# 160 instead of 128 tokens by gathered expert rows, the second expert product with its table rows stationary, and wide table tiles

## The chip, the cores and the metric

The kernel runs on one core of one Trainium2 chip. The metric is the device time of one execution in microseconds (us). Engines are named as in the profile: PE is TensorE, DVE VectorE, ACT ScalarE, POOL GpSimd, SP the queue of SyncE that issues the ordinary loads. GpSimd issues the gathers.

## What is computed

One layer of a decoder trunk on 512 tokens of 2048 features. A first part (norm, attention and linear attention heads, output projection) gives `x`. The second part is a mixture of 16384 experts of one neuron each, and a final norm:

```python
def peer_ffn(h, w_q, sub_keys, u_tab, v_tab):
    q = (h @ w_q).reshape(B, S, PEER_HEADS, 2, PEER_HALF)
    s = jnp.einsum('bshpd,hpkd->bshpk', q, sub_keys)
    top_s, top_i = lax.top_k(s, PEER_TOPK)
    ...
    expert = i1 * PEER_NKEYS + i2
    gate = jax.nn.softmax(best_s, axis=-1)
    ...
        u = jnp.take(u_tab, et, axis=0)
        act = jax.nn.gelu(jnp.einsum('td,ted->te', xt, u), approximate=False)
        return jnp.einsum('te,ted->td', gt * act, jnp.take(v_tab, et, axis=0))
```

Each token has 8 heads with 16 experts each, so 128 experts of the 16384. A row of `u_tab` and of `v_tab` is 2048 float32, 8 KB. The result is rmsnorm(x + g2 * peer_ffn(h)), with `g2` from the conditioning vector ("ada" sections below).

## The kernel before

**Two ways through the experts.** The first 128 tokens, one on each partition, go the gathered way. For each of their 128 expert slots GpSimd gathers 128 rows of `u_rows` (1 MB, one row for each token), VectorE multiplies them by the tokens' h and sums (`dot`), 16 slots at a time get gelu and gate (`weigh`), and then rows of `v_rows` are gathered, scaled and added up by VectorE (`add`). That makes 256 gathers, each followed by one VectorE instruction over 2048 columns. Three buffers `gat` go round. A gather is held back until ScalarE has cast a certain tile of `v_rows` (`pace[0]`).

The other 384 tokens go the dense way, through all 16384 experts, of which those that were not chosen have gate 0. The experts are taken in 128 groups of 128, a group being called j:

- `product1(j)` computes h times u for one j. Four table tiles of `u_t`, each 128x512 float32 (256 KB), are loaded by SP into `wraw` (six buffers). ScalarE casts each to its high part `whi`, VectorE subtracts to get the low part `wlo` (`split`; both have four buffers). TensorE then makes for each of 16 feature blocks three passes (high x high, high x low, low x high) with a 128x128 piece of the table stationary and the 384 tokens as moving columns: 48 passes of 384 columns. ScalarE's gelu puts the sum into `wt`.
- `gate(j)` multiplies `wt` by the dense gate matrix (`gtile`, read back from DRAM) on VectorE, casts the high part on ScalarE and subtracts the low part on VectorE.
- `product2(j, half)` multiplies these token weights by rows of the v table: the token weights are stationary (three blocks of 128 tokens) and 512 features move. For both halves of the features a j has 36 passes of 512 columns. Its v tiles are 128x512 too, loaded and split in the same way.

**The loop.** Chunks of `CH` = 4 j: for one half of the features, the four j are summed in six PSUM banks, then for the other half, and `evacuate` adds the six banks onto `xo` on VectorE; the half that ends a chunk stays in PSUM and begins the next chunk. Within every second step one more `product1` is made ahead (`next1`), and a step of the gathered way is taken (`sparse_some`). The engines' instruction streams are fixed when the program is built, by a scheduler that follows priorities and the buffers of the pools; on the chip every engine works through its own stream in order, and waits for semaphores.

**Around it.** Before the loop the top 16 of each head are found on VectorE, 14 first products are made ahead, and the dense gate matrix is generated in 12 blocks of 32 tokens: VectorE makes one-hot matrices, TensorE multiplies them, ScalarE copies them out (`stg`), and 2 MB of each block go to DRAM (`gd`). One section of the conditioning ("late ada", 64 tiles of 128x512 through `wraw`, summed by VectorE at L214) is worked off within the loop by `advance`. In the tail the last half is finished with v tiles split in advance (`stage`), GpSimd multiplies by `g2` and adds x (`onto_x1`, `other_half`), and the norm and the output follow token block by token block.

Of the kernel before, what the change touches and what calls it, by code (L numbers as in the profile page):

```python
# [21 lines left out]
P = 128  # L22
# [10 lines left out]
NDB = 3  # L33
NT = NDB * P
GT = 32
GJ = 4
CH = 4
NADA = 6
NWRAW = 6
# [3 lines left out]
RAW = 16  # L43
NPRE = 3
# [30 lines left out]
def hybrid_layer(ctx, tc, a, out):  # L75
# [49 lines left out]
    G1 = const.tile([P, KD], F32, name="G1")  # L125
    stat = const.tile([P, 5, 48], F32, name="stat")

    def rstd(dst, ss, n, width):
        v, y, z = stat[:, 1, :n], stat[:, 2, :n], stat[:, 3, :n]
# [25 lines left out]
    x1d = dram.tile([TB, P, D], F32, name="x1d")  # L155
# [496 lines left out]
    ws = pools.push("ws", LEFT, bufs=4)  # L652
# [20 lines left out]
    def first_heads(f):  # L673
        b = sums1[f] = bank(f"o{f // 2 % 2}")
        w = [load_w(ws, a["w_out"][f][:, k0:k0 + 4, :], [P, 4, P]) for k0 in (8, 12)]
        for ks, part, x in ((korder[:8], 0, mhi), (korder[:8], 1, mhi), (korder[:8], 0, mlo)):
            for k in ks:
                mm(b, w[k // 4 - 2][part][:, k % 4, :], x[k], start=x is mhi and part == 0 and k == 8, stop=False)

    for f in range(KD):  # L680
# [5 lines left out]
        for ik, k0 in enumerate((0, 4)):  # L686
            wh, wl = load_w(ws, a["w_out"][f][:, k0:k0 + 4, :], [P, 4, P])
            for j in range(4):
                mm3(b, wh[:, j, :], wl[:, j, :], mhi[k0 + j], mlo[k0 + j], False, k0 + j == 7)
            if f >= EWAIT:  # L690
                advance(2 + ik)
        x1f = x1T[:, f, :]
        nc.vector.scalar_tensor_tensor(out=x1f, in0=b, scalar=G1[:, f:f + 1], in1=x1f, op0=OP.mult, op1=OP.add)
        add_square(x1p, total, x1f, f == 0, nc.gpsimd if f < KD - 1 else nc.vector)
# [5 lines left out]
    h2 = [h2p.tile([P, TB, KD, P], F32R, name=n) for n in ("h2hi", "h2lo")]  # L700
# [4 lines left out]
    for k in range(KD):  # L705
# [3 lines left out]
        t4 = t.rearrange("p (a b) -> p a b", a=TB)  # L709
# [3 lines left out]
    for tb in range(TB):  # L713
        x1 = x1p.tile([P, D], F32, name="x1", tag="x1", bufs=2)
        for k4 in range(4):
            b = bank("tr")
            for j in range(4):
                nc.tensor.transpose(out=b[:, j * P:(j + 1) * P], in_=x1T[:, k4 * 4 + j, tb * P:(tb + 1) * P],
                                    identity=ident)
            nc.scalar.copy(out=x1[:, k4 * 512:(k4 + 1) * 512], in_=b)  # L720
        nc.sync.dma_start(out=x1d[tb], in_=x1)
# [6 lines left out]

    rp = pools.push("retr", RIGHT, bufs=2)
# [15 lines left out]
    for h in range(8):  # L745
        tv = rp.tile([P, 2, TB, 16], F32, name="tv", tag="tv")
        ti = rp.tile([P, 2, TB, 16], U32, name="ti", tag="ti")
        for p2 in range(2):
# [3 lines left out]
            b4 = b.rearrange("p (a b) -> p a b", a=TB)  # L752
            for k0 in range(0, KD, 4):
                wh, wl = load_w(ws, a["w_q"][f][:, k0:k0 + 4, :], [P, 4, P], "gpsimd")
                for j in range(4):
# [38 lines left out]
    def product1(j, lo_eng):  # L794
        b = bank("p1")
        b3 = b[:, :NT].rearrange("p (a b) -> p a b", a=NDB)
        wt = upl.tile([P, NT], F32, name="wt", tag="wt")
        for k0 in range(0, KD, 4):
# [9 lines left out]

    def next1(lo_eng="vector"):
        j = next(todo1, None)  # L810
# [15 lines left out]
    ef = slp.tile([P, P], F32, name="ef")  # L826
    flat = [[ids[:, tb, p2].rearrange("p h s -> p (h s)") for p2 in range(2)] for tb in range(TB)]
    nc.vector.scalar_tensor_tensor(out=ef, in0=flat[0][0], scalar=128.0, in1=flat[0][1], op0=OP.mult, op1=OP.add)
    nc.vector.tensor_copy(out=eidx, in_=ef)
    nc.vector.tensor_copy(out=gate0, in_=gates[:, 0].rearrange("p h s -> p (h s)"))  # L830
    slot = slp.tile([P, 4, NT], F16, name="slot")
    gres = slp.tile([P, NT], F32, name="gres")
    for tb in range(1, TB):
        for n, src in enumerate((flat[tb][0], flat[tb][1], gates[:, tb].rearrange("p h s -> p (h s)"))):
            b = bank("sk")
            nc.tensor.transpose(out=b[:, 0:P], in_=src, identity=ident)
            tsl = slice((tb - 1) * P, tb * P)
            if n == 2:
                nc.scalar.activation(gres[:, tsl], b[:, 0:P], AF.Copy, scale=GATE_UP)
            else:  # L840
                nc.scalar.copy(out=slot[:, n, tsl], in_=b[:, 0:P])
# [5 lines left out]
    for k4 in range(4):  # L847
        b = bank("pj")
        for j in range(4):
            k = k4 * 4 + j  # L850
            for n, src in enumerate(h2):
                mm(b[:, j * P:(j + 1) * P], src[:, 0, k, :], identr, start=(j == 0 and n == 0),
                   stop=(j == 3 and n == 1))
        nc.scalar.copy(out=h2s[:, k4 * 512:(k4 + 1) * 512], in_=b)
# [46 lines left out]
    act0 = sp.tile([P, P], F32, name="act0", bufs=1)  # L901
    wt0 = sp.tile([P, P], F32, name="wt0", bufs=1)
    nc.gpsimd.memset(acc0, 0.0)

# [298 lines left out]
```

## Time and profile before

| | |
|---|---|
| time, median of 3 runs (lowest to highest) | 3340.71 us (3340.18 to 3340.81) |
| profiled execution: its time, its span | 3344.42 us, 3342.7 us |
| busy in the span: PE, DVE, ACT, POOL | 95%, 75%, 37%, 27% |
| moved by DMA | 786.36 MB, 235 GB/s on average |
| granted TensorE clock, mean | 0.983 of full speed |

The span is what the profiler saw from the first instruction to the last. Busy times of TensorE overlap, since passes are pipelined: the distance between two starts is what a pass costs, not its duration. The other engines' instructions overlap slightly at their ends, too.

### The profile page before, as it was taken

To read this page: it belongs to the slowest core of one execution; us is meant where nothing else is said; L and a number is where in the kernel's file an instruction comes from. 1 tells how busy PE (TensorE), PEld (TensorE's weight loads), DVE (VectorE), ACT (ScalarE), POOL (GpSimd) and SP (SyncE) were. 2 spreads that over 40 slices of the span, in tenths; PEclk is the share of its full clock that TensorE was granted. 3 is DMA by queue.
4 is the path that set the end of the run, shared out by engine and by line. 5 is a ranking of instruction groups with operands and counts; after the bars stand their busy time and mean duration, and the time that the engine had idled before them with its cause. 6 is when DMAs were issued, how large, how long until landed. Compare 5 with 4: busy or idle time off the path is not lost. (4 is left out here: it accounts for less than half of the span.)

```text
span 3342.7 us, 46002 instructions
## 1 busy us (share of the span) xinstructions
PE 3173.7 (95%) x16009; PEld 2749.5 (82%) x16009; DVE 2523.7 (75%) x3989; ACT 1252.2 (37%) x2152; POOL 901.6 (27%) x630
## 2 busy tenths in 40 slices
PE   3999999999997889999999999999999999999997
PEld 2777786688786778988888888898888899999985
DVE  8988846674899885777777777777777777777777
ACT  3333354523422773333333333333333333333333
POOL 6554411111454462212211111112111111111123
PEclk9999999999998999999999999999999999999998
DMA  7876720184322468888888888888888888888864
GB/s 228 277 237 216 260 92 19 38 298 135 136 89 76 178 232 269 294 287 285 291 286 292 289 290 286 282 293 273 289 283 296 276 297 281 277 273 286 280 204 141
DMA packets 343817, 786.36 MB, mean 235 GB/s; under 512 B 33624, under 2 KB 108024, under 8 KB 307616
## 3 DMA queue, kind: packets, MB, share of 16 engines
q1 hardware_dynamic: 305600, 511.75, 47.3%
q0 software_dynamic: 37984, 271.68, 21.7%
q8 instruction: 125, 2.05, 0.2%
q14 instruction: 108, 0.88, 0.1%
HBM read 749.73 MB, written 33.56 MB: 234 GB/s over the span
## 5 line engine op out<-in xcount | busy, mean ns | idle before, releaser
L102 ACT CAST whi<-wraw 128x512 fp32r<-128x512 f32 (+1 forms) x779 | 477.2, 615 | 873.1 <-PE b_p L97 439.7
L97 PE MATMUL b_p<-h2hi,wlo 128*128 128x384 f32 x2048 | 695.0, 339 | 26.8 <-DVE wlo L103 19.7
L95 PE MATMUL b_p<-h2hi,whi 128*128 128x384 f32 x2048 | 692.6, 338 | 18.9 <-ACT whi L102 18.9
L96 PE MATMUL b_p<-h2lo,whi 128*128 128x384 f32 x2048 | 691.6, 338 | 0.0
L96 PE MATMUL b_p<-wlo,h2hi 128*128 128x512 f32 x1512 | 594.1, 393 | 10.7 <-DVE wlo L994 10.7
L97 PE MATMUL b_p<-whi,h2lo 128*128 128x512 f32 x1512 | 593.1, 392 | 0.0
L95 PE MATMUL b_p<-whi,h2hi 128*128 128x512 f32 x1512 | 589.5, 391 | 0.4 <-DVE xo L1022 0.2
L993 ACT CAST whi<-wraw 128x512 fp32r<-128x512 f32 x504 | 313.4, 623 | 684.8 <-PE b_p L96 537.1
L994 DVE TENSOR_TENSOR wlo<-wraw,whi 128x512 fp32r<-128x512 f32 x504 | 362.8, 725 | 273.4 <-ACT whi L993 271.5
L103 POOL TENSOR_TENSOR wlo<-wraw,whi 128x512 fp32r<-128x512 f32 (+1 forms) x259 | 410.8, 1595 | 416.7 <-ACT whi L102 385.8
L103 DVE TENSOR_TENSOR wlo<-wraw,whi 128x512 fp32r<-128x512 f32 x520 | 349.6, 689 | 124.9 <-ACT whi L102 124.5
L97 PEld LDWEIGHTS b_p<-h2hi,wlo 128*128 128x128 f32 x2048 | 386.8, 189 | 36.6 <-DVE wlo L103 27.4
L95 PEld LDWEIGHTS b_p<-h2hi,whi 128*128 128x128 f32 x2048 | 387.7, 189 | 24.2 <-ACT whi L102 19.2
L914 POOL DMA_INDIRECT gat<-in_u_rows,eidx x128 | 185.3, 1448 | 785.5 <-ACT whi L993 696.2
L96 PEld LDWEIGHTS b_p<-h2lo,whi 128*128 128x128 f32 x2048 | 387.2, 189 | 4.5
L914 POOL DMA_INDIRECT gat<-in_v_rows,eidx x128 | 161.9, 1265 | 802.5 <-ACT whi L993 688.5
L96 PEld LDWEIGHTS b_p<-wlo,h2hi 128*128 128x128 f32 x1512 | 285.2, 189 | 71.6 <-DVE wlo L994 14.5
L95 PEld LDWEIGHTS b_p<-whi,h2hi 128*128 128x128 f32 x1512 | 285.4, 189 | 61.6 <-issue 4.1
L97 PEld LDWEIGHTS b_p<-whi,h2lo 128*128 128x128 f32 x1512 | 285.4, 189 | 59.5
L214 DVE SCALAR_TENSOR_TENSOR acc<-adaw,cact,acc 128x512 f32<-128x512 f32 (+1 forms) x330 | 311.1, 965 | 22.4 <-DMA adaw<-in_ada_w 17.7
L928 DVE SCALAR_TENSOR_TENSOR acc<-gat,wt,acc 128x2048 f32<-128x2048 f32 x128 | 300.3, 2346 | 12.8 <-DMA gat<-in_v_rows,eidx 12.8
L920 DVE SCALAR_TENSOR_TENSOR gat<-gat,h2s 128x2048 f32<-128x2048 f32 x128 | 292.0, 2285 | 13.5 <-DMA gat<-in_u_rows,eidx 13.5
(359 smaller groups left out, 4185.2 us busy)
## 6 DMA issues: line engine op xcount, KB each, us to landing
wraw<-in_u_t SPq DMA_DIRECT2D x512, 256.0 KB, 4.2
wraw<-in_v_rows SPq DMA_DIRECT2D x512, 256.0 KB, 5.3
adaw<-in_ada_w SPq DMA_DIRECT2D x224, 256.0 KB, 4.3
adaw<-in_ada_w SPq DMA_DIRECT2D x128, 192.0 KB, 3.4
gd<-stg SPq DMA_DIRECT2D x12, 2048.0 KB, 7.3
gtile<-gd SPq DMA_DIRECT2D x32, 768.0 KB, 8.7
wraw<-in_w_out SPq DMA_DIRECT2D x64, 256.0 KB, 4.1
wraw<-in_w_q SPq DMA_DIRECT2D x64, 256.0 KB, 2.6
```

The lines of the kernel that those rows point to most:

```text
L95: mm(o, wh, xh, start=first, stop=False)
L96: mm(o, wh, xl, start=False, stop=False)
L97: mm(o, wl, xh, start=False, stop=last)
L102: nc.scalar.copy(out=hi, in_=src)
L103: (nc.vector if lo_eng == "vector" else nc.gpsimd).tensor_tensor(out=lo, in0=src, in1=hi, op=OP.subtract)
L214: nc.vector.scalar_tensor_tensor(out=acc, in0=w[:, j, :], scalar=cact[:, k:k + 1], in1=acc, op0=OP.mult, op1=OP.add)
L914: ins = nc.gpsimd.indirect_dma_start(out=g, out_offset=None, in_=a[table], in_offset=bass.IndirectOffsetOnAxis(ap=eidx[:, s:s + 1], axis=0))
L920: after(nc.vector.scalar_tensor_tensor(out=g, in0=g, scalar=1.0, in1=h2s, op0=OP.mult, op1=OP.mult, accum_out=act0[:, s:s + 1]), pace[1], ...
L928: after(nc.vector.scalar_tensor_tensor(out=acc0, in0=g, scalar=wt0[:, s:s + 1], in1=acc0, op0=OP.mult, op1=OP.add), pace[1], ORDER)
L993: pace[0] = nc.scalar.copy(out=vh, in_=vr).ins.name
L994: pace[1] = nc.vector.tensor_tensor(out=vl, in0=vr, in1=vh, op=OP.subtract).ins.name
```

## The change

- **Tokens.** 32 more tokens go the gathered way. Their slots are packed: 32 tokens on each quarter of the partitions, four of their 128 slots at once, so that they take 32 further slots of 128 rows (`eidxb`, `gateb`, `h2sb`, `accb`). That makes 160 slots and 320 gathers. The dense way has 352 tokens, in 11 groups of 32; h is stored in 16 groups of 32 tokens, so that the moving operand of `product1` is read in 11 runs of 32 columns, where it was read in 3 runs of 128.
- **Second product.** `product2(pair, g)` now holds 128x128 pieces of the v table stationary and moves the 352 token weights, as the first product does. The features are taken in four groups of 512 (`g`), each of four PSUM banks, and the result lies by features. A j has 48 passes of 352 columns here, and 96 in all.
- **Tiles.** All table tiles are 128x1024 (512 KB), of u, v (from a copy of the table in the order of its use, `v_t`), and of two projections ahead. `whi` and `wlo` have two buffers each, `wraw` three.
- **Loop.** Two chunks of four and twenty of six j; in each chunk four feature groups of two or three pairs, of which the first three are evacuated. 20 first products are made ahead of the loop.
- **Around it.** The gate matrix has 11 blocks. 16 copies on ScalarE put h of the gathered tokens in order. Only the 160 gathered tokens' x is transposed to rows. In the tail, x and `g2` are added on VectorE, blocks of the result are transposed back to rows, and the four copies of the 32 tokens are summed by a small matmul.

```diff
-NDB = 3
-NT = NDB * P
+NB = 32
+NA = P + NB
+NT = T - NA
+NQ = NT // GT
-CH = 4
+CHUNKS = (4, 4) + (6,) * 20
+NSLOT = 7
+NHOST = 8
+DG = 4
+PER1, PER2 = 1.42, 0.71
-NWRAW = 6
+NWRAW = 3
-RAW = 16
-NPRE = 3
+RAW = 12
+NPRE = 8
...
-    ws = pools.push("ws", LEFT, bufs=4)
+    ws = pools.push("ws", LEFT, bufs=2)
...
     def product1(j, lo_eng):
         b = bank("p1")
-        b3 = b[:, :NT].rearrange("p (a b) -> p a b", a=NDB)
-        wt = upl.tile([P, NT], F32, name="wt", tag="wt")
-        for k0 in range(0, KD, 4):
-            uh, ul = load_w(ws, a["u_t"][j][:, k0:k0 + 4, :], [P, 4, P], lo_eng)
-            for kk in range(4):
+        b3 = b[:, :NT].rearrange("p (a b) -> p a b", a=NQ)
+        wt = xo[:, j if j < DG else KD - NHOST + j, :] if j < NHOST else upl.tile([P, NT], F32, name="wt", tag="wt")
+        for k0 in range(0, KD, 8):
+            uh, ul = load_w(ws, a["u_t"][j][:, k0:k0 + 8, :], [P, 8, P], lo_eng)
+            for kk in range(8):
                 k = k0 + kk
-                mm3(b3, uh[:, kk, :], ul[:, kk, :], h2[0][:, 1:, k, :], h2[1][:, 1:, k, :], k == 0, k == KD - 1)
+                mm3(b3, uh[:, kk, :], ul[:, kk, :], h2[0][:, GA:, k, :], h2[1][:, GA:, k, :], k == 0, k == KD - 1)
...
-        for s0 in range(0, P, 16):
+        for s0 in list(range(P, NA, 16)) + list(range(0, P, 16)):
             for table, f in (("u_rows", dot), ("v_rows", add)):
...
+    def product2(pair, g, banks, first, last):
+        vr = ws.tile([P, 2, 512], F32, name="wraw", tag="wraw", bufs=NWRAW)
+        nc.sync.dma_start(out=vr, in_=a["v_t"][pair][g])
+        vh = ws.tile([P, 2, 512], F32R, name="whi", tag="whi")
+        vl = ws.tile([P, 2, 512], F32R, name="wlo", tag="wlo")
+        pace[0] = nc.scalar.copy(out=vh, in_=vr).ins.name
+        pace[1] = nc.vector.tensor_tensor(out=vl, in0=vr, in1=vh, op=OP.subtract).ins.name
+        for jj in range(2):
+            wh, wl = wpair[pair * 2 + jj]
+            for dc in range(DG):
+                dsl = slice(dc * P, (dc + 1) * P)
+                mm3(banks[dc][:, :NT], vh[:, jj, dsl], vl[:, jj, dsl], wh, wl, first and jj == 0, last and jj == 1)
+    def evacuate(g, banks):
+        for dc in range(DG):
+            o = xo[:, g * DG + dc, :]
...
+                nc.vector.tensor_tensor(out=o, in0=banks[dc][:, :NT], in1=o, op=OP.add)
...
+    for c, n in enumerate(CHUNKS):
+        order = range(DG) if c % 2 == 0 else range(DG - 1, -1, -1)
...
+        for p, g in enumerate(order):
...
+            for i in range(n // 2):
+                if step % 2 == 1:
+                    n1 = done1[0]
+                    next1()
+                    sparse_some(PER1 * (done1[0] - n1))
+                if c > 1 and step % 2 == 0:
+                    advance()
+                product2(j0 // 2 + i, g, banks, i == 0 and (p > 0 or c == 0), i == n // 2 - 1 and
+                         (p < DG - 1 or c == last_c))
+                if p == DG - 1 and c < last_c:
+                    gate(j0 + n + CHUNKS[c + 1] * (i + 1) // (n // 2) - gated[0])
+                sparse_some(PER2)
+                step += 1
...
+            elif p < DG - 1:
+                evacuate(g, banks)
```

Where instructions stand is shown at two places. The first is VectorE's stream in the loop, around an evacuation. Before, it reads so (`wlo` of L994 is a v tile's low part and of L103 a u tile's; L928 adds a gathered slot; L1022 evacuates a bank onto `xo`):

```order
L994 TENSOR_TENSOR wlo_22540<-wraw_22537,whi_22539 128x512
L928 SCALAR_TENSOR_TENSOR acc0_11141<-gat_22408,wt0_11143,acc0_11141 128x2048
L994 TENSOR_TENSOR wlo_22570<-wraw_22567,whi_22569 128x512
L994 TENSOR_TENSOR wlo_22585<-wraw_22582,whi_22584 128x512
L1022 TENSOR_TENSOR xo_11146<-b_p2_21956,xo_11146 128x512
L1022 TENSOR_TENSOR xo_11146<-b_p2_21957,xo_11146 128x512
L1022 TENSOR_TENSOR xo_11146<-b_p2_21958,xo_11146 128x512
L1022 TENSOR_TENSOR xo_11146<-b_p2_21959,xo_11146 128x512
L1022 TENSOR_TENSOR xo_11146<-b_p2_21960,xo_11146 128x512
L1022 TENSOR_TENSOR xo_11146<-b_p2_21961,xo_11146 128x512
L928 SCALAR_TENSOR_TENSOR acc0_11141<-gat_22441,wt0_11143,acc0_11141 128x2048
L103 TENSOR_TENSOR wlo_22610<-wraw_22607,whi_22609 128x512
```

The first v tile of this piece ends the six banks' sums; the two after the slot's addition belong to the next step.

In the changed kernel the same place reads so (L1031 and L113 are the low parts of v and u tiles, L972 adds a slot, L1017 multiplies by the gates, L1046 evacuates):

```order
L1031 TENSOR_TENSOR wlo_19355<-wraw_19352,whi_19354 128x1024
L1031 TENSOR_TENSOR wlo_19388<-wraw_19385,whi_19387 128x1024
L972 SCALAR_TENSOR_TENSOR acc0_10961<-gat_19346,wt0_10964,acc0_10961 128x2048
L1017 TENSOR_TENSOR wt_19284<-wt_19284,gtile_19992 128x352
L972 SCALAR_TENSOR_TENSOR acc0_10961<-gat_19349,wt0_10964,acc0_10961 128x2048
L1046 TENSOR_TENSOR xo_7121<-b_p2_18988,xo_7121 128x352
L1046 TENSOR_TENSOR xo_7121<-b_p2_18989,xo_7121 128x352
L1046 TENSOR_TENSOR xo_7121<-b_p2_18990,xo_7121 128x352
L1046 TENSOR_TENSOR xo_7121<-b_p2_18991,xo_7121 128x352
L113 TENSOR_TENSOR wlo_19431<-wraw_19428,whi_19430 128x1024
L113 TENSOR_TENSOR wlo_19461<-wraw_19458,whi_19460 128x1024
```

Both v tiles here belong to the sums that are evacuated. The next tile of TensorE is a u tile, and its low part stands behind the four evacuations; the low parts that stood ahead of them for the next step are not there any more.

The second place is ScalarE's stream ahead of the gate generation, where h of the gathered tokens is made (`h2s`, from PSUM) and the first blocks of gates are copied out (`stg`). Before:

```order
L839 ACTIVATE gres_9677<-b_sk_9702 128x128
L854 COPY h2s_9711<-b_pj_9712 128x512
L854 COPY h2s_9711<-b_pj_9722 128x512
L854 COPY h2s_9711<-b_pj_9732 128x512
L854 COPY h2s_9711<-b_pj_9742 128x512
L891 ACTIVATE stg_9764<-b_gg_9773 128x4x128
L891 ACTIVATE stg_9764<-b_gg_9783 128x4x128
L891 ACTIVATE stg_9764<-b_gg_9801 128x4x128
L891 ACTIVATE stg_9764<-b_gg_9811 128x4x128
```

In the changed kernel `hc` are copies of h in another order, two for each piece of `h2s` and, further on, of `h2sb`:

```order
L868 ACTIVATE gres_9534<-b_sk_9559 128x128
L885 COPY hc_9574<-h2hi_6962 128x512
L885 COPY hc_9580<-h2lo_6963 128x512
L885 COPY hc_9588<-h2hi_6962 128x512
L885 COPY hc_9594<-h2lo_6963 128x512
L885 COPY hc_9602<-h2hi_6962 128x512
L889 COPY h2s_9568<-b_pj_9573 128x512
L885 COPY hc_9608<-h2lo_6963 128x512
L885 COPY hc_9616<-h2hi_6962 128x512
L889 COPY h2s_9568<-b_pj_9587 128x512
L885 COPY hc_9622<-h2lo_6963 128x512
```

Sixteen such copies and four more pieces now stand ahead of the first `stg`.

## Rows read from the trace of the kernel before

**Rows 1.** Busy time, share of the span and instructions of TensorE and its weight loads.
```profile
PE 3173.7 (95%) x16009; PEld 2749.5 (82%) x16009; DVE 2523.7 (75%) x3989; ACT 1252.2 (37%) x2152; POOL 901.6 (27%) x630
```

**Rows 2.** Windows: start and end, length, busy by engine, granted clock, DMA share, GB/s.
```profile
2000.00:2300.00 300.00, 293.75 (x1477) 264.16 (x1476) 217.24 (x277) 102.86 (x178) 54.22 (x38) 1.00 0.83 286
2405.00:2413.00 8.00, 8.00 (x38) 6.67 (x37) 3.71 (x4) 3.30 (x6) 2.08 (x2) 1.00 1.07 389
2416.00:2419.40 3.40, 3.30 (x10) 3.30 (x11) 3.14 (x7) 0.00 (x0) 0.00 (x0) 0.51 0.57 171
2900.00:3200.00 300.00, 300.00 (x1523) 273.67 (x1522) 218.78 (x267) 104.41 (x180) 48.52 (x39) 1.00 0.81 276
```

**Rows 3.** Timeline of TensorE: start, duration, pass, and idle time ahead of it.
```profile
1271.38 0.40 PE L95 MATMUL b_p<-whi,h2hi 128*128 128x512 f32 x1
...
2399.84 0.33 PE L96 MATMUL b_p<-h2lo,whi 128*128 128x384 f32 x1
...
2405.39 0.39 PE L95 MATMUL b_p<-whi,h2hi 128*128 128x512 f32 x1
...
2413.59 0.33 PE L95 MATMUL b_p<-h2hi,whi 128*128 128x384 f32 x1
...
2416.10 0.69 PE L97 MATMUL b_p<-h2hi,wlo 128*128 128x384 f32 x1 [2.00 <-DVE wlo L103]
...
2419.47 0.35 PE L95 MATMUL b_p<-h2hi,whi 128*128 128x384 f32 x1
```

**Rows 4.** TensorE's groups from 3193 on: count, busy, mean ns, idle before.
```profile
L96 PE MATMUL b_p<-wlo,h2hi 128*128 128x512 f32 x149 | 61.5, 413 | 9.2 <-DVE wlo L994 9.2
...
L95 PE MATMUL b_p<-h2hi 128*128 128x512 f32 x24 | 9.3, 389 | 0.0
```

**Rows 5.** Instructions of one line: min/median/max ns, first and last start.
```profile
L803 ACT ACTIVATE wt<-b_p x128: 479/488/578, 1044.7 to 3192.9; 128x384 f32<-128x384 f32 x128
L891 ACT ACTIVATE stg<-b_gg x96: 1063/1144/1226, 1095.1 to 1241.8; 128x512 f32<-128x512 f32 x96
L718 PE MATMUL b_tr<-ident,x1T x64: 270/273/331, 829.6 to 845.7; 128*128 128x128 f32 x64
```

**Rows 6.** Chain of waits, 1400 to 3200: who, for whom, us, times, longest.
```profile
POOL gat L914 <- ACT whi L993: 1280.3, 186, 15.3
...
DVE acc L214 <- DMA wraw<-in_ada_w: 112.1, 36, 6.5
...
PE b_p L97 <- DVE wlo L103: 18.8, 18, 2.6
```

**Rows 7.** Timeline of VectorE, 2412 to 2430.
```profile
2412.62 2.35 DVE L928 SCALAR_TENSOR_TENSOR acc<-gat,wt,acc 128x2048 f32<-128x2048 f32 x1 [4.29 <-DMA gat<-in_v_rows,eidx]
...
2417.57 0.69 DVE L103 TENSOR_TENSOR wlo<-wraw,whi 128x512 fp32r<-128x512 f32 x1
2418.17 0.55 DVE L977 TENSOR_TENSOR wt<-wt,gtile 128x384 f32<-128x384 f32 x1
2418.64 0.55 DVE L982 TENSOR_TENSOR h2lo<-wt,h2hi 128x384 fp32r<-128x384 f32 x1
...
2422.86 2.35 DVE L928 SCALAR_TENSOR_TENSOR acc<-gat,wt,acc 128x2048 f32<-128x2048 f32 x1
2425.12 0.69 DVE L994 TENSOR_TENSOR wlo<-wraw,whi 128x512 fp32r<-128x512 f32 x1
...
2429.88 0.75 DVE L214 SCALAR_TENSOR_TENSOR acc<-wraw,cact,acc 128x512 f32<-128x512 f32 x1
```

**Rows 8.** DMA issues: count, KB each, median us from issue to landing.
```profile
gat<-in_u_rows,eidx POOLq DMA_INDIRECT x128, 8.5
gat<-in_v_rows,eidx POOLq DMA_INDIRECT x128, 8.4
```

**Rows 9.** The page's costliest groups: count, busy, mean ns, idle before.
```profile
L993 ACT CAST whi<-wraw 128x512 fp32r<-128x512 f32 x504 | 313.4, 623 | 684.8 <-PE b_p L96 537.1
```

**Rows 10.** Timeline of VectorE in the tail.
```profile
3267.11 0.68 DVE L994 TENSOR_TENSOR wlo<-wraw,whi 128x512 fp32r<-128x512 f32 x1
...
3271.30 4.73 DVE L994 TENSOR_TENSOR wlo<-wraw,whi 128x512 fp32r<-128x512 f32 x2
```

More of the change, by code (lines that the diff above doesn't have):

```diff
@@ L685, in hybrid_layer @@
             nc.sync.dma_start(out=x1T[:, f:f + 2, :], in_=a["x_t"][:, f:f + 2, :])
[L686 to L694, printed above, removed]
+        wh, wl = load_w(ws, a["w_out"][f][:, 0:8, :], [P, 8, P])
+        for j in range(8):
+            mm3(b, wh[:, j, :], wl[:, j, :], mhi[j], mlo[j], False, j == 7)
+            if f >= EWAIT and j % 4 == 3:
+                advance(2 + j // 4)
+        xf = x1T[:, f, :]
+        nc.vector.scalar_tensor_tensor(out=xf, in0=b, scalar=G1[:, f:f + 1], in1=xf, op0=OP.mult, op1=OP.add)
+        add_square(x1p, total, xf, f == 0, nc.gpsimd if f < KD - 1 else nc.vector)
     advance(1000)
@@ L699, in hybrid_layer @@
     h2p = pools.push("h2", LEFT)
-    h2 = [h2p.tile([P, TB, KD, P], F32R, name=n) for n in ("h2hi", "h2lo")]
+    h2 = [h2p.tile([P, NG, KD, GT], F32R, name=n) for n in ("h2hi", "h2lo")]
     ss = bank("m")
@@ L712, in hybrid_layer @@
                                        op0=OP.add, op1=OP.subtract)
-    for tb in range(TB):
+    nc.sync.dma_start(out=x1f, in_=x1T[:, :, NA:])
+    for t0, m, dst in ((0, P, x1a), (P, NB, x1b)):
         x1 = x1p.tile([P, D], F32, name="x1", tag="x1", bufs=2)
@@ L1010, in new_banks @@
-    def new_banks():
-        return [[bank("p2") for _ in range(NDB)] for _ in range(2)]
-    fresh = [True, True]
-    def evacuate(half, banks):
-        for nb in range(2):
-            for tb in range(NDB):
-                o = xo[:, half, tb, nb * 512:(nb + 1) * 512]
-                if fresh[half]:
-                    nc.scalar.copy(out=o, in_=banks[nb][tb])
-                else:
-                    nc.vector.tensor_tensor(out=o, in0=banks[nb][tb], in1=o, op=OP.add)
-        fresh[half] = False
@@ new lines, in combine @@
+    def combine():
+        sel = fin.tile([P, NB], F32, name="sel")
+        nc.vector.tensor_tensor(out=sel, in0=ident[:, 0:NB], in1=ident[:, NB:2 * NB], op=OP.add)
+        for q in range(2, QB):
+            nc.vector.tensor_tensor(out=sel, in0=sel, in1=ident[:, q * NB:(q + 1) * NB], op=OP.add)
+        for k4 in range(4):
+            sl = slice(k4 * 512, (k4 + 1) * 512)
+            b = bank("p1")
+            mm(b[:NB, :], sel, accb[:, sl], start=True, stop=True)
+            nc.scalar.copy(out=accb[:NB, sl], in_=b[:NB, :])
@@ L1034, in hybrid_layer @@
+    for _ in range(RAW + NHOST - NPRE):
         next1("gpsimd")
     load_gates(0)
-    for j in range(CH):
-        gate(j)
-    NCH = P // CH
-    late = chain(mod_row(ws, 5, g2d, c * 512, 512, "p1") for c in range(4))
-    for c in range(NCH):
-        halves = (0, 1) if c % 2 == 0 else (1, 0)
-        if c == NCH - 1:
+    gate(CHUNKS[0])
+    late = chain(mod_both(c * 512, 512) for c in range(4))
+    ready = []
+    step = 0
+    j0 = 0
+    last_c = len(CHUNKS) - 1
+    for c, n in enumerate(CHUNKS):
+        order = range(DG) if c % 2 == 0 else range(DG - 1, -1, -1)
+        if c == last_c:
+            for _ in late:
+                pass
+            for _ in sparse:
+                pass
```

338 lines of the change are left out of this document (174 added, 164 removed).

## The prediction

> **What bounds the kernel now.** I read the busy shares first. TensorE is busy 95% of the span [rows 1], so the question is what its passes cost, and what makes it wait. The windows come next: from 2900 to 3200 us it has no free microsecond, from 2000 to 2300 it lacks 6, and VectorE is busy 72% in both [rows 2]. So the expert loop is bound by TensorE, with VectorE some way behind and the DMA at 276 to 286 GB/s.
>
> For the price of a pass I take the distance from start to start in the timeline, since matmuls overlap. Between 2399.84 and 2405.39 stand 32 passes of 384 columns, 0.1734 us each; between 2405.39 and 2413.59 stand 36 of 512, 0.2278 each [rows 3]. One group of 128 experts (one j) has 48 of the first kind and 36 of the second: 8.32 + 8.20 = 16.52 us.
>
> What does TensorE lose in the loop today? It runs from the first second-product pass at 1271.38 [rows 3] to the last gelu at 3192.9 [rows 5], 1921.5 us. In it lie 114 first products (14 are made ahead of it) and 4088 passes of 512 columns (4608, less 448 of the table and 72 of the staged tiles that come after 3193; three lines of about 149 and of 24 [rows 4]). 114 x 8.32 + 4088 x 0.2278 = 1880. So some 42 us are lost. The chain of waits names VectorE's low part of the next u tile for 18 of the gaps, 18.8 us together [rows 6]. One such gap is in the timeline: VectorE idles 4.29 us for gathered rows, adds them at 2412.62 [rows 7], and only then makes the low part that TensorE needs; the pass at 2416.10 starts after 2.00 us idle, and 10 passes from there take 3.37 us where they take 1.73 otherwise [rows 3]. The granted clock of that stretch is 0.51, the lower of the two levels (1.2 of 2.4 GHz), and 1.00 before and after [rows 2].
>
> **The change, part by part.**
>
> *Passes.* A j now has 96 passes of 352 columns. The trace has none. By the slope between the two kinds, 0.0544 us for 128 columns, one takes 0.1734 - 0.0136 = 0.160 us. The bounds are 0.159 (in proportion to the columns) and 0.1734 (no faster than 384, since the moving operand is read in runs of 32 columns). I take 0.160, because both measured kinds lie on one line, and the 384 columns were read in three runs too. 96 x 0.160 = 15.35 us, 1.17 less; over 128 j **-150 us** (-162 to +16 by the bounds).
>
> *VectorE's load.* Its issue distances are 0.60 us for 512 columns (2417.57 to 2418.17), 0.47 for 384 (to 2418.64), 2.26 for a gathered slot of 2048 (2422.86 to 2425.12) [rows 7]: about 1.03 ns a column. So 352 columns take 0.435 and 1024 take 1.13. Today a j holds 8 low parts (4.8), 2.24 slots (5.06), one gate pair (0.94) and 1.5 evacuated banks (0.9): 11.7 of 16.52, 71%, which the 72% of the window bear out. Now it holds 4 wide low parts (4.52), 2.84 slots (6.42; 320 slots of rows where 256 were), a gate pair (0.87) and 2 banks (0.87): 12.7 of 15.35, 83%, and 13.4 or 87% where a late ada tile (0.75 [rows 7]) falls into each j. VectorE stays below TensorE on average, but its free time falls from 4.8 to 2.7 us a j, and with ada tiles from 4.1 to 2.0.
>
> *New fixed stalls.* In the order, after four evacuations VectorE makes the low part of the very tile that TensorE wants next, while the two hi/lo buffers hold what came before. TensorE's last pass of the group must end before the last bank is evacuated: 0.435 for the bank, then 1.13 for the low part, less 0.32 for the two passes that need the high part alone, make 1.25 us. The signals between the engines come on top; I take 1.5, between this and the gap of 2.00. Before, two v tiles' low parts stood ahead of the evacuation, and these fed TensorE for 4 us. This place comes twice in a chunk of six j. Where the chunk changes, three gates and two slots come together, for some 1.4 us by the same walk. 4.5 us x 20 chunks = 90; the floor, the two hard places alone, is 60.
>
> *Late ada tiles.* VectorE waits 36 times for them, 112.1 us, 3.1 each [rows 6]. The free 4.1 us of a j cover that today; the 2.0 of the new one leave 1.1 open: 36 x 1.1 = 40. (Between 0 and 112.) They also take one of now three table buffers, each of 512 KB, which two v tiles share with them. Gaps near 2 us cost the clock, 1.64 us in the one above; I add 10 for some six of them. So the loop loses 90 + 40 + 10 = 140 where it lost 42: **+98** (+18 with the floor alone, +170 with the whole 112).
>
> *Gathers.* One every 5.4 us where it was one every 7.4. They land after 8.5 us [rows 8]; with 1.4 to issue and 2.26 to be used, a ring of three goes round in 12.2, and has 16.2. GpSimd waits 1280 us for its pace now [rows 6], so it has the time. I charge nothing; the cover is 4 us a gather.
>
> *Ahead of the loop.* One block fewer of gate generation, of twelve that take 1095.1 to 1241.8 [rows 5]: -12.2. Sixteen copies of 512 columns on ScalarE, at the cast's 0.62 [rows 9], in front of it: +10. The 20 first products made early instead of 14 are the same passes at another place. 32 of 64 transposes fewer, which took 829.6 to 845.7 [rows 5]: -8 if they keep that pace, 0 if something else sets it; I take -4. Together **-6** (-20 to +15). The wide tiles of the output and query projections do the same passes; 0.
>
> *The tail.* VectorE's low parts take 2.4 us each where GpSimd's additions run beside them (two in 4.73 us, one 0.69 elsewhere) [rows 10], and TensorE waits 9.2 us for them [rows 4]. These additions move to VectorE. What is left behind the last pass is alike: transposes and a norm. **-9** (0 to -20).
>
> The profiled execution took 3344.4 us, 1.7 more than its span. 3344.4 - 150 + 98 - 6 - 9 = 3277.4; the runs' median of 3340.7 is 3.7 below the profiled one, so **3274 us**.
>
> **The rivals.**
> *A, only the hard stalls stay* (60 in the chunks, ada hidden): 3274 - 80 = 3194. For it: VectorE's average has room, and from 2900 to 3200, without ada tiles, nothing is lost. Against: 36 waits for ada today.
> *B, slower: gathered rows come late.* VectorE works in order, so a late slot holds the low part behind it, as at 2412.62. With 2.84 slots a j and 2.4 us free, lateness of 0.85 us a slot is hidden; at 1.2 us each of 113 j loses 1.0, +114, which gives 3388. It passes the old time from 1.06 us on (+67). The ring has 4 us of slack, so the landing would have to go from 8.5 to some 13.7. For it: the loop's bytes, 108 u and 128 v j of 1.05 MB, 320 gathers of 1.05, gates 22 and ada 17, are 622 MB in some 1810 us, 344 GB/s where it is 286 now. Against: stretches of 389 GB/s at full clock, as 2405 to 2413 [rows 2].
> *C, the DMA stays at 286 GB/s*: 622 MB take 2175 us, 365 more than the loop has, 3639. Against it the same row of 389, at which the bytes take 1600. The Trainium skill ("DMA: Bandwidth & Descriptors", Specifications) gives about 358 GB/s as a core's share of the memory; by that the bytes take 1737 us, an estimate, and the loop would still be TensorE's, with 4% to spare. The 389 of the row is above that share, so the trace does not bear it out as a limit here.
> *D, 352 columns in eleven runs go no faster than 384*: -150 becomes +16, 3440.
>
> **How the numbers follow.** My case has 0.50, A 0.17, B 0.24, C 0.03, D 0.06. The predicted time is my case's, with 3225 to 3325 as its own range. From 3190 to 3392 leaves out the lower end of A, half of B, and C and D, about 2 in 10. 0.2% is 6.7 us, about what a measurement of this kernel can tell from no change: my case and B's lower end put 0.06 within it; faster 0.67, slower 0.27.
>
> **What would show it.** Starts 0.160 us apart in the new loop, else the first term falls (0.173 is D). Gaps of about 1.5 us ahead of a u tile after evacuations, twice in 90 us, with VectorE's low part as what ended them; no such gaps would be A. VectorE near 85% in the loop; slots idling on gathered rows for over 1 us on average would be B, with landings of 13 us. DMA near 344 GB/s; below 300 it is C. I would be wrong above all in the stalls, which were walked by hand from the order of instructions and which no row shows.

## The result, and the profile of the changed kernel

The changed kernel takes 3456.59 us (median of 4 runs, 3448.51 to 3464.40) where the kernel before takes 3340.76: a ratio of 1.0345, with an interval of 1.0314 to 1.0376. It is slower by 116 us; the forecast was 3274, faster, with a range that ended at 3392.

The profiled execution took 3448.51 us with a span of 3446.6. Busy shares first:

```profile
PE 3133.1 (91%) x17569; PEld 2864.9 (83%) x17569; DVE 2574.2 (75%) x3632; ACT 1143.7 (33%) x1594; POOL 980.1 (28%) x631
```

TensorE is busy 41 us less than before, and 91% of the span where it was 95% [rows 1]. The windows, in the columns of [rows 2], the last two around one gap:

```profile
2000.00:2300.00 300.00, 274.05 (x1578) 267.14 (x1577) 221.09 (x221) 83.19 (x103) 67.14 (x46) 0.95 0.83 302
2900.00:3200.00 300.00, 275.64 (x1636) 271.26 (x1635) 218.26 (x207) 85.28 (x104) 71.81 (x48) 0.97 0.81 300
2995.20:3001.00 5.80, 5.78 (x20) 5.78 (x21) 1.54 (x2) 0.00 (x0) 0.00 (x0) 0.50 0.53 185
3001.50:3009.00 7.50, 7.50 (x48) 7.50 (x48) 5.89 (x5) 2.95 (x4) 3.59 (x2) 1.00 0.51 170
```

The same for the whole stretch from 1400 to 3200, first of the kernel before and then of the changed one:

```profile
1400.00:3200.00 1800.00, 1780.76 (x8970) 1610.64 (x8969) 1325.84 (x1649) 622.07 (x1077) 323.71 (x239) 1.00 0.83 285
1400.00:3200.00 1800.00, 1653.72 (x9713) 1618.48 (x9713) 1337.19 (x1309) 505.08 (x615) 418.70 (x286) 0.97 0.83 304
```

Where TensorE had no free time from 2900 to 3200, it now lacks 24 us of 300, and 26 in the stretch with ada tiles. From 1400 to 3200 it is free for 146 us in place of 19, and its mean granted clock falls from 1.00 to 0.97. VectorE stands at 73 to 74%, hardly above the 72% of before: it has not become full. The loop runs at 300 GB/s; 344 were expected.

TensorE's timeline: the first second-product pass of the loop, a u tile and a v tile in full flow, the gap of 2995 and the end of the stretch at half clock behind it, and the last second-product pass.

```profile
1340.58 0.32 PE L105 MATMUL b_p<-h2hi,whi 128*128 128x352 f32 x1
...
2602.25 0.32 PE L106 MATMUL b_p<-h2lo,whi 128*128 128x352 f32 x1
...
2609.49 0.32 PE L105 MATMUL b_p<-h2hi,whi 128*128 128x352 f32 x1
...
2611.41 0.32 PE L105 MATMUL b_p<-h2hi,whi 128*128 128x352 f32 x1
...
2991.18 0.32 PE L106 MATMUL b_p<-h2lo,whi 128*128 128x352 f32 x1
2995.22 0.66 PE L107 MATMUL b_p<-h2hi,wlo 128*128 128x352 f32 x1 [3.72 <-DVE wlo L113]
...
3000.96 0.35 PE L105 MATMUL b_p<-h2hi,whi 128*128 128x352 f32 x1
...
3428.50 0.32 PE L107 MATMUL b_p<-h2hi,wlo 128*128 128x352 f32 x1
```

From 2602.25 to 2609.49 lie 44 passes of the first product, 0.1645 us each; from there to 2611.41 twelve of the second, 0.160 each. So a j costs 48 x 0.1645 + 48 x 0.160 = 15.58 us, 0.94 less than the 16.52 of before.

What VectorE did ahead of the gap that ends at 2995.22:

```profile
2984.49 1.23 DVE L1031 TENSOR_TENSOR wlo<-wraw,whi 128x1024 fp32r<-128x1024 f32 x1 [0.51 <-ACT whi L1030]
2985.63 2.29 DVE L962 SCALAR_TENSOR_TENSOR gat<-gat,h2s 128x2048 f32<-128x2048 f32 x1
...
2990.01 2.29 DVE L962 SCALAR_TENSOR_TENSOR gat<-gat,h2s 128x2048 f32<-128x2048 f32 x1 [2.08 <-DMA gat<-in_u_rows,eidx]
...
2992.22 1.81 DVE L1046 TENSOR_TENSOR xo<-b_p,xo 128x352 f32<-128x352 f32 x4
2993.95 2.35 DVE L113 TENSOR_TENSOR wlo<-wraw,whi 128x1024 fp32r<-128x1024 f32 x2
```

Between the low part of the last v tile (from 2984.49) and that of the u tile TensorE wants (to about 2995.1) stand two slots, 2.08 us of waiting for rows, and four banks: 10.6 us from start to end. TensorE passes a tile in 3.9 us, and there are two buffers. The same kind of place stands in the order that was shown ahead of the prediction. In this gap the late rows weigh most: without these 2.08 us some 1.6 of the 3.72 would be left, an estimate.

The waits from 1400 to 3200, in the columns of [rows 6]:

```profile
PEld b_p L107 <- DVE wlo L113: 156.4, 74, 4.7
DVE acc L227 <- DMA wraw<-in_ada_w: 148.4, 58, 4.8
PE b_p L107 <- DVE wlo L113: 135.5, 72, 4.4
...
DVE gat L962 <- DMA gat<-in_u_rows,eidx: 23.7, 21, 2.6
...
DVE acc L972 <- DMA gat<-in_v_rows,eidx: 18.5, 18, 2.4
```

The passes' wait for a u tile's low part has gone from 18.8 us in 18 times [rows 6] to 135.5 in 72; the first line is the same wait as the weight loads (PEld) see it. Sorted by what stands on VectorE between the late low part and the table tile's low part before it, the 72 gaps are:

| in between on VectorE | gaps | us lost | VectorE's wait for gathered rows in there, us |
|---|---|---|---|
| slots and the four banks of an evacuation | 33 | 85 | 21 |
| slots and three instructions of `gate` | 11 | 26 | 10 |
| slots and at most one other instruction | 28 | 25 | 14 |

In 69 of the 72 two slots stand there, and in 38 VectorE has waited for their rows. Gathered rows land no later than before [rows 8]:

```profile
gat<-in_u_rows,eidx POOLq DMA_INDIRECT x128, 8.2
gat<-in_v_rows,eidx POOLq DMA_INDIRECT x128, 8.0
```

**Where the 104 us of the span come from.** Ahead of the loop, beside its first products: 1340.6 - 20 x 7.90 = 1182.7, against 1271.4 - 14 x 8.32 = 1154.9, +28. In the loop, from the first to the last second-product pass: 2087.9 us, of which the passes need 108 x 7.90 + 6144 x 0.160 = 1836, so 252 are lost; before, by the same count up to its last pass at 3328.4, 2057.0 - 1998.2 = 59; +193. Of the 252 the timeline shows 155 as free time in 89 gaps, and 56 as what 32 stretches of 8 to 20 passes at half clock lose; some 20 more go in single slower passes, and the rest is not accounted for. Passes: 128 x -0.94 = -121. After the last pass: 18.1 against 14.3, +4. Together +104.

### The profile page after: what moved, and what is told of

It reads as the page before. It is cut to its first block, busy times and chain, and to the rows that moved or that the text cites. A ratio compares the mean times of both kernels' runs of the same rounds, so it can differ in the third digit from the quotient of the medians.

```text
span 3446.6 us, 45915 instructions
## 1 busy us (share of the span) xinstructions
PE 3133.1 (91%) x17569; PEld 2864.9 (83%) x17569; DVE 2574.2 (75%) x3632; ACT 1143.7 (33%) x1594; POOL 980.1 (28%) x631
## 5 line engine op out<-in xcount | busy, mean ns | idle before, releaser
L107 PE MATMUL b_p<-h2hi,wlo 128*128 128x352 f32 x4096 | 1372.6, 336 | 164.5 <-DVE wlo L113 144.4
L105 PE MATMUL b_p<-h2hi,whi 128*128 128x352 f32 x4096 | 1362.4, 333 | 28.8 <-ACT whi L112 23.2
L106 PE MATMUL b_p<-h2lo,whi 128*128 128x352 f32 x4096 | 1355.7, 331 | 0.0
L107 PEld LDWEIGHTS b_p<-h2hi,wlo 128*128 128x128 f32 x4096 | 793.4, 194 | 192.2 <-DVE wlo L113 166.8
L105 PEld LDWEIGHTS b_p<-h2hi,whi 128*128 128x128 f32 x4096 | 794.1, 194 | 36.8 <-ACT whi L112 23.9
L106 PEld LDWEIGHTS b_p<-h2lo,whi 128*128 128x128 f32 x4096 | 793.2, 194 | 0.1
L112 ACT CAST whi<-wraw 128x1024 fp32r<-128x1024 f32 (+2 forms) x459 | 414.3, 905 | 968.2 <-PE b_p L106 440.2
L1030 ACT CAST whi<-wraw 128x1024 fp32r<-128x1024 f32 x256 | 268.8, 1050 | 918.7 <-PE b_p L106 839.1
L1031 DVE TENSOR_TENSOR wlo<-wraw,whi 128x1024 fp32r<-128x1024 f32 x256 | 313.2, 1223 | 303.8 <-ACT whi L1030 303.4
L113 POOL TENSOR_TENSOR wlo<-wraw,whi 128x512 fp32r<-128x512 f32 (+3 forms) x211 | 404.5, 1924 | 472.3 <-ACT whi L112 442.8
L113 DVE TENSOR_TENSOR wlo<-wraw,whi 128x1024 fp32r<-128x1024 f32 x248 | 298.2, 1217 | 31.0 <-ACT whi L112 30.2
L972 DVE SCALAR_TENSOR_TENSOR acc<-gat,wt,acc 128x2048 f32<-128x2048 f32 x128 | 300.3, 2346 | 20.1 <-DMA gat<-in_v_rows,eidx 19.9
L227 DVE SCALAR_TENSOR_TENSOR acc<-wraw,cact,acc 128x512 f32<-128x512 f32 x60 | 45.1, 751 | 148.4 <-DMA wraw<-in_ada_w 148.4
L1046 DVE TENSOR_TENSOR xo<-b_p,xo 128x352 f32<-128x352 f32 x236 | 106.9, 514 | 0.2 <-PE b_p L107 0.2
```

The lines of the kernel that those rows point to most:

```text
L105: mm(o, wh, xh, start=first, stop=False)
L106: mm(o, wh, xl, start=False, stop=False)
L107: mm(o, wl, xh, start=False, stop=last)
L112: nc.scalar.copy(out=hi, in_=src)
L113: (nc.vector if lo_eng == "vector" else nc.gpsimd).tensor_tensor(out=lo, in0=src, in1=hi, op=OP.subtract)
L227: nc.vector.scalar_tensor_tensor(out=acc, in0=w[:, j, :], scalar=cact[:, k:k + 1], in1=acc, op0=OP.mult, op1=OP.add)
```

## The experiments

The theories. **Theory 1**: VectorE works in order, and slots and evacuations stand ahead of a u tile's low part, which TensorE wants with its third pass. **Theory 2**: the DMA, with 320 gathers beside the tables and three raw buffers, brings tiles or rows too late. **Theory 3**: VectorE lacks throughput. A single run of the changed kernel may lie 8 us to either side of its median.

**1. The low part's passes last** (the second product in the same way):

```diff
-                mm3(b3, uh[:, kk, :], ul[:, kk, :], h2[0][:, GA:, k, :], h2[1][:, GA:, k, :], k == 0, k == KD - 1)
+                mm(b3, uh[:, kk, :], h2[0][:, GA:, k, :], start=k == 0, stop=False)
+                mm(b3, uh[:, kk, :], h2[1][:, GA:, k, :], start=False, stop=False)
+            for kk in range(8):
+                k = k0 + kk
+                mm(b3, ul[:, kk, :], h2[0][:, GA:, k, :], start=False, stop=k == KD - 1)
```

> Within each wide tile all 16 passes with the high part of the table come first and the 8 with the low part last; the same 24 passes. Theory 1 (VectorE's order: gathered slots and evacuations stand ahead of the first u tile's low part, and TensorE wants it with its third pass): the low part is wanted 2.6 us into the tile instead of 0.33, so the 77 gaps on it (169 us) shrink to under 40 and most of the passes at half clock (58 us) go: about 3280 us, 3250 to 3310. Theory 2 (the DMA is too slow for 320 gathers beside the tables) and theory 3 (VectorE lacks throughput): the gaps come back in front of high parts or further on; 3420 to 3460.

Measured: 3354.83 us, ratio to before 1.0033 (1.0014 to 1.0052). 102 us go, where theory 1 had said 147 to 207. From 1400 to 3200 TensorE's free time falls from 146 to 93 us, and the stretches at half clock from 30 to 15. The waits now (same stretch):

```profile
ACT whi L1034 <- DMA wraw<-in_v_t: 436.0, 98, 13.0
...
ACT whi L112 <- DMA wraw<-in_u_t: 192.6, 74, 6.4
DVE acc L227 <- DMA wraw<-in_ada_w: 148.1, 54, 8.5
...
PEld b_p L823 <- DVE wlo L113: 32.2, 25, 4.9
```

The wait for the low part falls from 156 to 32 us, and ScalarE now waits for table tiles from the DMA (43 and 69 us in the changed kernel): a second limit, hidden behind the first.

**2. The evacuation behind the next first product's tiles.**

```diff
                     next1()
+                    for e in held:
+                        evacuate(*e)
+                    held.clear()
...
             elif p < DG - 1:
-                evacuate(g, banks)
+                if step % 2 == 1:
+                    held.append((g, banks))
+                else:
+                    evacuate(g, banks)
```

The next group's banks are taken behind that first product, too.

> The evacuation that is followed by a first product is issued after that product's tiles, so that the u tile's low part stands ahead of the four banks on VectorE; same work. Theory 1: two gaps in a chunk lose the 1.7 us of the evacuation, with the clock 70 to 110 us in all: 3345 to 3385. Theories 2 and 3: within 20 us of 3450.

Measured: 3392.31 us, 64 less; a little short of the expectation, of theory 1's size.

**3, 4. No gathered way**, in the changed kernel and in the one before:

```diff
-    sparse = sparse_steps()
+    nc.vector.memset(act0, 0.0)
+    sparse = iter(())
```

> The changed kernel without the gathered way in the loop (no gathers, no slot instructions on VectorE; the first 160 tokens lack their experts). Theory 1: the gaps left are those of the evacuations alone, 20 chunks x 2 x 1.5: lost 60 to 80 where 255 were lost, 3265 to 3285. Theory 2 and theory 3: lost under 20 us, 3215 to 3235.

> The kernel before without the gathered way in the loop (the first 128 tokens lack their experts). All theories: of its 42 lost us at most 30 go, 3305 to 3335; if it falls by more than 60, the gathered way was already dear before, and its price in the changed kernel is not new.

Measured: 3215.78 and 3321.18 us. The gathered way costs the kernel before 24 us (3345.61 by the runs of this comparison) and the changed one 241. Theory 1 in its narrow form, with gaps that evacuations make by themselves, is refuted: without slots TensorE is never free in the stretch shown below. The time without slots is where theories 2 and 3 had put it, so it does not tell whether the slots are dear by VectorE's time or by their gathers; 5 and 6 take these apart.

```profile
2000.00:2300.00 300.00, 300.00 (x1849) 298.26 (x1848) 138.13 (x168) 95.39 (x115) 0.00 (x0) 1.00 0.51 162
```

**5, 6. Slots without VectorE's time, and without gathers.**

```diff
-        after(nc.vector.scalar_tensor_tensor(out=g, in0=g, scalar=1.0, in1=of(s, h2s, h2sb)[0], op0=OP.mult,
+        after(nc.vector.scalar_tensor_tensor(out=g[:, 0:128], in0=g[:, 0:128], scalar=1.0, in1=of(s, h2s, h2sb)[0][:, 0:128], op0=OP.mult,
...
-        after(ins, pace[0], SYNC)
-        return g
...
+        ring.append(ring.pop(0))
+        return resident[ring[0] % len(resident)]
```

> The changed kernel with all 320 gathers, but VectorE's instruction for a slot takes 128 of the 2048 columns (the gathered tokens come out wrong). The gathered way cost 241 us in the changed kernel (3457 to 3216). Theory 1 (VectorE's time for the slots, in front of low parts): over 170 of these go, below 3285. Theory 2 (the gathers' DMA and the waiting for rows): under 70 go, above 3385.

> The opposite: VectorE's slot instructions at their full 2048 columns, on three tiles that stay in place, and no gathers (the gathered tokens come out wrong). Theory 1: over 150 of the 241 us stay, above 3365. Theory 2: under 80 stay, below 3295. If both this and the one with short slots are fast, neither alone is dear, and it is the two together: late rows that hold up a stream which is nearly full.

Measured: 3497.36 with short slots, slower than the changed kernel itself, and 3339.17 with resident ones, so that VectorE's instructions alone keep 123 of the 241 us. That lies between the two expectations: the other 117 go with the gathers, that is with late rows, with loads that come later beside them, or with both. The gaps on low parts without gathers:

```profile
PE b_p L107 <- DVE wlo L113: 79.8, 70, 2.2
```

They are as many as before, and shorter. The answer of the short slots goes against theory 1 as it stood. Its trace shows why (VectorE, then the queue of SP, whose second row is the issue of the same ada tile):

```profile
2048.25 1.22 DVE L113 TENSOR_TENSOR wlo<-wraw,whi 128x1024 fp32r<-128x1024 f32 x1 [1.74 <-ACT whi L112]
2056.70 0.75 DVE L227 SCALAR_TENSOR_TENSOR acc<-wraw,cact,acc 128x512 f32<-128x512 f32 x1 [7.23 <-DMA wraw<-in_ada_w]
2057.37 1.22 DVE L113 TENSOR_TENSOR wlo<-wraw,whi 128x1024 fp32r<-128x1024 f32 x1
```

```profile
2045.67 0.33 SPq L1027 DMA_DIRECT2D wraw<-in_v_t  x1
2049.50 0.33 SPq L221 DMA_DIRECT2D wraw<-in_ada_w  x1
```

All three raw buffers are taken until the low part at 2048.25 frees one. Only then is the ada tile issued, at 2049.50; VectorE has nothing else in front, reaches the ada instruction at once and waits 7.23 us for it, and the low part of the next u tile stands behind. With full slots VectorE comes to the ada tiles later, and waits 148.4 us for them in 58 times, as shown above; with short ones it waits more than twice as long:

```profile
DVE acc L227 <- DMA wraw<-in_ada_w: 320.5, 60, 9.3
```

**7. Without the late ada section, and 8. with short slots besides.**

```diff
-    late = chain(mod_both(c * 512, 512) for c in range(4))
+    nc.vector.memset(G2, 1.0)
+    nc.sync.dma_start(out=g2d, in_=h2s[0:1, :])
+    late = iter(())
```

> The changed kernel without the late ada section (g2 is wrong). The prediction gave it 40 us plus clock. By the windows of the changed kernel, which lose 26 of 300 us with and without ada tiles, it should be little: theory 1 3420 to 3450. If late ada tiles in a third of the raw buffers are the main loss (theory 2 by that way): below 3390.

> Short slot instructions, all 320 gathers, and no late ada section (outputs wrong in both). With short slots alone the time rose to 3497, and VectorE waited 320 us for ada tiles, up to 9 at a time, with low parts queued behind. If that wait is the whole of it, the time falls by 150 or more, below 3345. If the gathers delay the tables by themselves, it stays above 3420, since no_ada alone gave 45.

Measured: 3411.62 and 3235.39 us. So with full slots the ada section costs 45 us, with short ones 262; without it, the slots' time on VectorE costs 176. The 45 lie between the two expectations for 7. All 320 gathers run in the last kernel, and it is within 20 us of the one that has none (and has the ada tiles): the gathers' traffic is not dear by itself (theory 2 in that form is out). The 117 of experiment 6 come only where the slots fill VectorE besides.

**9. Gathers without their pace** (the line `after(ins, pace[0], SYNC)` left out).

> The changed kernel with gathers issued as soon as a buffer is free, without the wait for ScalarE's cast. Theory 1 with late rows: VectorE's 47 us of waits for rows, which lie just ahead of evacuation and low part, go: 20 to 60 us less, 3395 to 3435. If the rows were late because the DMA is full: no change, or slower by bursts, 3440 to 3490.

Measured: 3449.43 us, no change. The waits from 1400 to 3200:

```profile
ACT whi L1029 <- DMA wraw<-in_v_t: 213.7, 49, 8.4
DVE acc L227 <- DMA wraw<-in_ada_w: 202.7, 55, 8.3
...
PE b_p L107 <- DVE wlo L113: 107.7, 71, 4.1
...
DVE acc L971 <- DMA gat<-in_v_rows,eidx: 0.5, 1, 0.5
```

VectorE's waits for rows are gone, and the gaps on u tiles' low parts are 28 us less. But v tiles come later (ScalarE waits 214 us for them where it waited 43), and ada tiles too. Earlier gathers only move the loss; what late rows cost by themselves is not shown by this run.

**10, 11. Both reorderings, and a fourth raw buffer** (12 is the buffer alone).

```diff
-NWRAW = 3
+NWRAW = 4
-RAW = 12
+RAW = 10
...
-            sq = fin.tile([P, 512], BF16, name="sqf", tag="sqf", bufs=2)
+            sq = fin.tile([P, 512], BF16, name="sqf", tag="sqf", bufs=1)
```

> Both reorderings together: low-part passes last, and the evacuation behind the next first product's tiles. Theory 1: the 32 us of gaps on evacuated banks and most of the 30 on low parts go, 3355 to some 3310 (3290 to 3330). Theory 2 (what is left is table tiles that come late through three raw buffers, 37 us on high parts and their clock): no gain or little, 3340 to 3360.

> The same with four raw table buffers where three were (and 18 first products ahead in place of 20, to make room). Theory 2: the high parts come in time, 30 to 50 us less than without. Theory 1: within 10 us of it.

> The changed kernel with a fourth raw table buffer alone (18 first products ahead in place of 20, one buffer less in the tail). Theory 2 (three raw buffers of 512 KB make table tiles late beside 320 gathers; the low part on VectorE is only the last to come): 80 to 110 us less, as the fourth buffer gave on the reordered kernel, 3345 to 3380. Theory 1 (VectorE's order sets the gaps, and the buffer helps only once the order is mended): 3420 to 3455.

Measured: 3363.65 (1.0058, 1.0038 to 1.0077), 3260.19 (0.9756, 0.9723 to 0.9790), and for the buffer alone 3442.02 (1.0295, 1.0266 to 1.0324). On three buffers the later evacuation adds nothing to the low part last; a fourth buffer then takes off 103 us, and taken alone 15. The two limits lie behind each other. The buffer alone does mend the ada waits, and little comes of it:

```profile
PEld b_p L107 <- DVE wlo L113: 162.4, 82, 7.4
...
DVE acc L227 <- DMA wraw<-in_ada_w: 26.3, 12, 9.3
```

In the reordered kernel with four buffers the DMA carries 340 GB/s and TensorE loses 6 of 300 us, or 1 where no ada tiles come; VectorE is busy 82 to 83% there, so theory 3 is out:

```profile
2000.00:2300.00 300.00, 294.35 (x1800) 291.16 (x1799) 248.63 (x247) 93.60 (x113) 84.07 (x53) 0.99 0.93 340
2700.00:3000.00 300.00, 299.13 (x1848) 298.25 (x1848) 247.28 (x235) 96.83 (x115) 70.59 (x55) 1.00 0.92 337
```

**13, 14. The low part last and four buffers, evacuations left alone; and 3 first products ahead of the gates** (`NPRE = 3` where 8 stood).

> Low-part passes last and four raw buffers, evacuations where the changed kernel has them. On three buffers the later evacuation brought nothing (3355 without, 3364 with it). If what is left hangs on raw buffers and not on VectorE's order: within 10 us of 3260; if the order still counts with four buffers: 3280 to 3310.

> The same, with 3 first products ahead of the gate generation in place of 8, as the kernel before has. The time ahead of the loop rose by 28 us beside its first products, 12 of them in the stretch with the gates; if the 5 more products there (39 us, TensorE at 0.83 clock, 70% busy) are what delays the gates, 10 to 25 us less than without; else within 8.

Measured: 3269.48 (0.9773, 0.9748 to 0.9797) and 3256.69 us (0.9743, 0.9722 to 0.9764). The evacuation's place is worth 9 us, within the scatter of the runs. 13 us lie between the two medians, but the intervals overlap, and the traces do not put them down to the five products: with 3 ahead of the gates the first second-product pass starts at 1325.8, with 8 at 1331.3 here and at 1317.6 in the kernel of experiment 11, which has the same first part. The copies of the gates (`stg`) start earlier, at 1134.6 where they start at 1175.2 and 1163.5, but the first products that were put off then follow them.

**15. The kernel before with its low parts last**, in both products.

> The kernel before with the same reordering as the changed kernel got (passes with the table's low part last in each tile). It loses 42 us in its loop, 19 of them on u tiles' low parts: 10 to 30 us less, 3310 to 3335. If more, the reordering is worth as much without the change.

Measured: 3317.98 us, ratio 0.9921 (0.9890 to 0.9951). So the reordering is worth 26 us without the change and 102 with it, and the change with its three mends is some 60 us ahead of that too.

**16. One run of 352 columns** in the first product:

```diff
-                mm3(b3, uh[:, kk, :], ul[:, kk, :], h2[0][:, GA:, k, :], h2[1][:, GA:, k, :], k == 0, k == KD - 1)
+                x0, x1 = [h[:, GA:].rearrange("p g k t -> p (g k t)")[:, k * NT:(k + 1) * NT] for h in h2]
+                mm3(b3, uh[:, kk, :], ul[:, kk, :], x0, x1, k == 0, k == KD - 1)
```

> The first product reads 352 columns in one run instead of 11 of 32 (other columns of the same tile, so the output is wrong). If the runs cost the 5 ns by which a pass of the first product is dearer (0.1646 against 0.1595), starts come 0.1595 apart and up to 31 us go, some into waits: 3425 to 3450; else no change in the distance.

Measured: 3473.99 us, one run. The distance did fall; between these two rows of a u tile's timeline lie 42 passes, 0.161 each:

```profile
2700.55 0.33 PE L107 MATMUL b_p<-h2hi,wlo 128*128 128x352 f32 x1
...
2707.32 0.33 PE L107 MATMUL b_p<-h2hi,wlo 128*128 128x352 f32 x1
```

The time did not: where VectorE sets the pace of the low parts, faster passes are only followed by longer gaps (153 us on low parts from 1400 to 3200, where it was 136). Why this run is 17 us above the median stays open.

## Why the prediction was wrong

The error of 183 us, by the prediction's own steps:

- *Passes*, forecast -150, measured -121. The second product's distance was right (0.160); the first product's is 0.1645, since its columns come in 11 runs of 32. That such runs might cost was seen as a bound and given to rival D, as all or nothing. "Both measured kinds lie on one line" was no ground against it, as two points always do. +29.
- *New fixed stalls*, *Late ada tiles* and the tail's gain, forecast +98 - 9, measured +193. **This is the step that failed**, in the stalls and in what they cost the clock. "1.25 us. The signals between the engines come on top; I take 1.5": the walk began with the evacuation of the last bank, as if the two slots in front were done by then, with their rows in time. The order that it quoted shows two slots and a gate there, and the rows show 2.3 us for each slot. The gaps behind an evacuation came to 2.6 us each in place of 1.5, those at the three gates to 2.4 in place of 1.4, and 28 of 0.9 came at places that the prediction did not have. That the place was right is shown by experiments 1 and 2, which change only the order; that the slots were what was left out, by 3, 6 and 8. VectorE's average load, which the prediction worked out as 83%, said nothing on it: the changed kernel stands at 73 to 74% and loses 24 to 26 of 300 us, the mended one at 82 to 83% and loses 1 to 6.
- Within that step the clock is the term that was furthest off: "10 for some six" gaps. From 1400 to 3200 the timeline shows 30 stretches of 11 to 20 passes at half clock, 29 of them behind a gap on a u tile's low part, such as the 19 passes from 2995.22 that take 5.74 us where 3.1 are usual. Each loses 1.7 us, close to the 1.64 that the prediction took, and together they lose 52, 56 in the whole loop. Stalls and ada tiles together were forecast at 130 us of free time, and 155 were measured; so near by luck, as the parts were not right.
- *Gathers*, forecast 0. The landing did stay at 8.0 to 8.2 us, but in 38 of the 72 gaps VectorE had waited for rows, 45 us in all. The prediction's sum asked only whether the ring of three has slack on average. What this cost is not shown by itself: taking the gathers away gives 117 us, issuing them earlier gives nothing.
- *Late ada tiles*, forecast 40, measured 45 by leaving them out. The agreement is luck: the size hangs on what else delays VectorE (262 with short slots), and the mechanism that the prediction mentioned in passing, a third of the raw buffers, is the one that the trace of the short slots shows.
- *Ahead of the loop*, forecast -6, measured +28. 16 of these lie ahead of the first of the first products (1048.8, before 1033.0); that point scatters, and lies at 1051.7 and 1063.4 in the kernels of experiments 11 and 13, whose first parts are alike. The query projection, which moves 512 columns in 16 runs of 32, is dearer by some 7 of them (its passes stand 0.237 apart, 0.227 before). The other 12 lie from there to the loop, in the stretch with the gates. That the five more products ahead of the gates cause these is not borne out by experiment 14. The rest stays open. +34.
- After the last pass +4, and the runs' median lies 8 above the profiled execution where it lay 4 below: +16 together.

The rivals: A is refuted by the result, but holds for the mended kernel (6 and 1 us lost of 300). B, late rows, gave the sign, and its mechanism is there, as a slot that waits holds the low part behind it; but not its size or its cause: rows land after 8.0 to 8.2 us, not 13, and VectorE waits some 48 us for them from 1400 to 3200, 0.2 a slot. C is out, since 340 GB/s are reached once TensorE takes the tiles. D held in part.

What is shown is that two limits stand behind each other: the place of the u tile's low part in VectorE's stream, and the ring of three raw buffers, which the ada tiles share. Mending the first alone gives 102 us, the second alone 15, both 187. Of what is lost from 1400 to 3200 in the changed kernel, 146 us are waits themselves and 52 the half clock behind them. What is open is how much of the waits is the slots' own 2.3 us and how much their late rows, and what part the two wide buffers for high and low parts have: no run changed their number.

## What to carry to other kernels

Before costing a change by an engine's average load, add up what stands in its order between two things that the bound engine waits for, and hold this against the work that the buffers between them cover. Leaving out the gathered way, with its slots of 2.3 us, gave 24 us in the kernel before and 241 in the changed one. Where one operand of a split product comes late, run the passes that don't need it first: it cost nothing here and gave 102 us. And if a mend brings little, look whether another limit has taken its place before giving it up: the fourth buffer was worth 15 us or 85. A test that takes one wait away can bring another, as the earlier gathers did: look at the waits as well as at the time.

## What the runs showed of the hardware that was not expected

A pass that reads its 352 moving columns in 11 runs of 32 takes 0.1645 us, in one run 0.160 to 0.161. Giving VectorE less to do (short slots) made the kernel 41 us slower, since it then ran into its loads earlier, in order. The half clock (granted clock 0.50) came behind some gaps and not behind others: of the 72 on low parts, the 24 of up to 1.2 us were followed by no such stretch, and of the 48 of 1.4 us and more 29 were and 19 were not, one of these 3.4 us long. Some stretches began with the first pass after the gap, others about 1 us later.
